# Seven block products in place of eight for half of a down projection's columns, with weight sums made by accumulating DMAs and interleaved with the up projection

## The chip, the core and the metric

The kernel runs on one core of a Trainium2 chip. The metric is the time that the device takes for one execution, in microseconds (us). The profile below is of one such execution, and its times count from the first instruction of the span.

## What is computed

Two decoder layers over 256 tokens of width 2048, all in 32-bit floats. Each layer is a mixer, a convolutional FFN and a gated per-layer embedding, each with a norm ahead of it. The change is in the FFN, which is the larger part of the work:

```python
def conv_ffn(hn, w_up, conv_w, conv_b, w_down):
    u = causal_dwconv(hn @ w_up, conv_w) + conv_b   # w_up 2048 x 11264, conv over 3 tokens
    gate, up = jnp.split(u, 2, axis=-1)
    return (jax.nn.silu(gate) * up) @ w_down        # w_down 5632 x 2048

for i in range(DEPTH):                              # DEPTH 2
    h = h + mixers[i](rmsnorm(h, attn_norms[i]))
    ...
    h = h + conv_ffn(rmsnorm(h, ffn_norm), w_up, conv_w, conv_b, w_down)
```

The mixer of layer 0 matters too, since the change moves buffers that it uses: its first projection (width 5200) gives, in a narrow piece near the start, the two gate inputs of the delta-rule heads (8 columns each), from which `gates()` makes beta and the decay.

## The kernel before

**Precision.** A product of two 32-bit matrices is made of three products of rounded parts: both operands are cut into `hi` (a cast to the rounded form) and `lo` (the rest), and hi·hi, hi·lo and lo·hi are added up in PSUM. A weight chunk of 1 MB comes by one DMA on SP's queue into one of RAWB = 3 `raw` buffers (`load`, L156 to 164), and `split` (L166) cuts it in two pieces of 128x1024: ACT makes `hi` (L179) and DVE makes `lo` = raw − hi (L180). There are WB = 4 buffers each of `hi` and of `lo`. The activations are cut the same way and kept in tiles called `xg`.

**Two gemms.** `gemm_b` (L243 to 260) holds the weights as the stationary operand: a chunk of 8 blocks of 128 by 256 columns takes 16 matmuls of 512 columns (hi against both parts of x, L252), and after a `yield` 16 of 256 columns (lo, L257). The up projection uses it: two chunks for each 256 of its columns. `gemm_a` (L269 to 290) holds the tokens: a chunk of 4 blocks of 128 by 512 columns takes 16 matmuls of 512 columns (L281 and L282, hi) and 8 (L287, lo). The down projection uses it through `proj_add` (L345), which adds the result to the residual tiles `h` on DVE (L351).

**The FFN** (`ffn`, L907) goes by groups of 128-wide blocks of the 44 that d_ff has: (0,4), (4,12), (12,20), (20,28), (28,36), (36,44). For a group, `up` makes two `conv` per pair of blocks: `gemm_b`, then ACT copies the PSUM result (L264) and DVE scales it (L265, L267), ACT makes the first tap of the convolution (L924), DVE adds two taps for each half (L926), and after both, ACT makes silu (L935), DVE multiplies (L936), and ACT and DVE cut the product into `xg` (L356, L357). After a group's `up` stands the whole down projection of the group before it. The last group's down projection comes at the end.

**Order.** Every engine runs its own instructions in an order that is fixed when the program is built: a scheduler orders them from the written program and its dependencies. The pools of buffers (`raw`, `hi`, `lo`, `xg`, PSUM `pa` and `pb`, and T2B = 27 tiles `t` of 128x512) add the waits: a new user of a buffer waits for the last reader of the old one.

**Start of layer 0.** The constants (`cst`, 770.5 KB) and the gates' small tensors (`ab`, `beta`, `gdec`, `eg`, `kdx`, `nbe`) have memory of their own. The narrow piece of the first projection is in PSUM after the first of the gemms of 368 columns, ACT scales it out (L441), and `gates()` follows with three exponentials (L463, L468, L475), a logarithm and another exponential (L484, L488), each of the last two behind a load of ACT's function table.

Of the kernel before, what the change touches and what calls it, by code (L numbers as in the profile page):

```python
# [21 lines left out]
P = 128  # L22
# [7 lines left out]
RAWB = 3  # L30
WB = 4
PSA = 2
PSB = 4
RATES = [1.7, 1.1, 1.1, 0.95, 2.8]
# [48 lines left out]
def trunk(ctx: ExitStack, tc: tile.TileContext, a: dict):  # L83
# [52 lines left out]
    cst = cp.tile([P, N_CST], F32, name="cst", tag="cst")  # L136
# [217 lines left out]

    def put_split(t, k, n, src):
        A.copy(t[:, k : k + n, 0], src)  # L356
        V.tensor_sub(t[:, k : k + n, 1], src, t[:, k : k + n, 0].bitcast(F32))  # L357
# [77 lines left out]
    ab = cp.tile([P, NH, 16], F32, name="ab", tag="ab")  # L435
# [11 lines left out]
    beta = cp.tile([P, HEADS, NH], F32, name="beta", tag="beta")  # L447
    gdec = cp.tile([P, HEADS, NH], F32, name="gdec", tag="gdec")
    eg = cp.tile([P, HEADS, NH], F32, name="eg", tag="eg")
    kdx = cp.tile([P, HEADS, NH], F32, name="kdx", tag="kdx")  # L450
    nbe = cp.tile([P, HEADS, NH], F32, name="nbe", tag="nbe")
# [91 lines left out]
    kp = [cp.tile([P, S], F32, name=f"kp{j}", tag=f"kp{j}") for j in range(2)]  # L543
# [364 lines left out]
    def ffn(l, nf, nxt, aside=None):  # L908
# [9 lines left out]
        def conv(cb, j0):  # L918
            ps = run(gemm_b(w_up, cb, Xf))
# [9 lines left out]
        def up(g0, g1):  # L929
            tiles = []  # L930
            for jp in range(g0, g1, 2):
                tiles.append(xtile())
                yg = conv(jp * P, jp)
                yu = conv(D_FF + jp * P, NFT + jp)
# [3 lines left out]
            return tiles  # L938
# [3 lines left out]
        for g0, g1 in groups:  # L942
            cur = up(g0, g1)
# [4 lines left out]
            if prev is not None:  # L948
                run(proj_add(w_dn, [(prev[0] * P, prev[2], prev[1] - prev[0])], range(CG)))
            prev = (g0, g1, cur)  # L950
# [43 lines left out]
    px = ffn(0, n, ng, lambda: rope_tables(cst[:, C_IRET : C_IRET + 1], cos_r, sin_r, None))  # L994
# [297 lines left out]
```

## Time and profile before

| what | before |
|---|---|
| median of three runs (range) | 2904.06 us (2902.49 to 2905.63) |
| the profiled execution | 2901.51 us |
| its span | 2899.7 us |
| mean granted TensorE clock | 0.999 |
| TensorE busy | 2882.3 us, 99% of the span |
| VectorE (DVE) busy | 1933.0 us, 67% |
| ScalarE (ACT) busy | 1470.1 us, 51% |
| GpSimd (POOL) busy | 64.8 us, 2% |
| DMA | 528.91 MB, mean 182 GB/s |

PE is TensorE's matmuls, PEld its weight loads, which lie beside the matmuls. A mean duration of an instruction includes its latency: instructions of one engine overlap, so their starts stand closer together than their durations. L numbers are lines of the kernel before; in the changed kernel they are moved by 7 at first and by 101 to 133 after `proj_add`.

### The profile page before, as it was taken

What the parts mean: (1) busy time and instruction counts of PE and PEld (TensorE: products, weight loads), DVE (VectorE), ACT (ScalarE), POOL (GpSimd) and SP (SyncE); (2) the same over time, 40 slices, a digit from 0 to 9 for tenths busy, and PEclk for the clock granted to TensorE, in tenths of its full rate; (3) what the DMA queues carried; (4) which work ended last, traced back from release to release, by engine and by line L of the source; (5) the groups of instructions that cost most, each with busy time, mean ns of one, the idle gap of its engine ahead of it and who ended that gap; (6) DMA issues with size and microseconds to landing.
All of it is one profiled execution on the core that took longest, in us unless ns stands there. A gap on an engine that the chain in (4) does not pass through costs nothing.

```text
span 2899.7 us, 38285 instructions
## 1 busy us (share of the span) xinstructions
PE 2882.3 (99%) x15172; PEld 2483.8 (86%) x15172; DVE 1933.0 (67%) x2697; ACT 1470.1 (51%) x2105; POOL 64.8 (2%) x68
## 2 busy tenths in 40 slices
PE   9999999999999999999999999999999999999998
PEld 9899988888888888888888888888888888888887
DVE  7878767777676766556656565665677767666665
ACT  7666645555454544554444443444554544445454
POOL 0111100000000000000000000000000000000000
PEclk9999999999999999999999999999999999999999
DMA  7444355555556555555555555555555555555554
GB/s 241 128 132 141 128 167 182 189 189 189 192 187 198 196 189 191 176 187 187 181 186 183 191 180 186 184 184 189 178 190 192 189 196 189 189 194 188 194 181 162
DMA packets 392117, 528.91 MB, mean 182 GB/s; under 512 B 9216, under 2 KB 265344, under 8 KB 391936
## 3 DMA queue, kind: packets, MB, share of 16 engines
q1 hardware_dynamic: 388512, 521.66, 55.3%
q10 hardware_dynamic: 3424, 4.79, 0.5%
q8 instruction: 119, 1.95, 0.3%
q14 instruction: 62, 0.51, 0.1%
HBM read 524.32 MB, written 2.10 MB: 182 GB/s over the span
## 4 chain that ended last, share of the span: by engine, by line
PE 97%; DVE 1%; DMA 1%; ACT 1%; issue 0%; POOL 0%; ACTq 0%; POOLq 0%; SPq 0%; DVEq 0%
PE pa L252 30%; PE pa L257 16%; PE pa L281 15%; PE pa L282 15%; PE pa L287 14%; PE pb L591 2%; PE pb L301 1%; PE pa L788 1%; DVE lo L180 0%; PE pb L597 0%; PE pb L1031 0%; ACT hi L179 0%; PE pb L233 0%; PE pb L231 0%; PE pb L230 0%
## 5 line engine op out<-in xcount | busy, mean ns | idle before, releaser
L180 DVE TENSOR_TENSOR lo<-raw,hi 128x1024 fp32r<-128x1024 f32 (+3 forms) x1140 | 1200.8, 1075 | 674.3 <-ACT hi L179 614.8
L179 ACT CAST hi<-raw 128x1024 fp32r<-128x1024 f32 (+3 forms) x1140 | 1015.7, 931 | 1087.4 <-PE pa L282 503.9
L252 PE MATMUL pa<-xg,hi 128*128 128x512 f32 x3840 | 927.8, 392 | 0.0
L252 PEld LDWEIGHTS pa<-xg,hi 128*128 128x128 f32 x3840 | 704.5, 188 | 135.6
L281 PE MATMUL pa<-hi,xg 128*128 128x512 f32 (+1 forms) x1924 | 746.6, 388 | 1.0 <-ACT hi L179 1.0
L282 PE MATMUL pa<-hi,xg 128*128 128x512 f32 (+1 forms) x1924 | 744.6, 387 | 0.0
L257 PEld LDWEIGHTS pa<-xg,lo 128*128 128x128 f32 x3840 | 490.3, 191 | 16.3
L257 PE MATMUL pa<-xg,lo 128*128 128x256 f32 x3840 | 502.0, 283 | 0.0
L287 PE MATMUL pa<-lo,xg 128*128 128x512 f32 (+1 forms) x1924 | 473.7, 387 | 0.0
L281 PEld LDWEIGHTS pa<-hi,xg 128*128 128x128 f32 x1924 | 361.7, 188 | 71.3 <-ACT hi L179 1.3
L282 PEld LDWEIGHTS pa<-hi,xg 128*128 128x128 f32 x1924 | 361.5, 188 | 70.1
L287 PEld LDWEIGHTS pa<-lo,xg 128*128 128x128 f32 x1924 | 358.3, 188 | 70.2
L926 DVE SCALAR_TENSOR_TENSOR t<-t,fp,t 128x255 f32<-128x255 f32 (+1 forms) x352 | 161.7, 481 | 108.3 <-ACT t L924 105.2
L264 ACT COPY t<-pa 128x512 f32<-128x512 f32 x128 | 75.1, 587 | 76.8 <-PE pa L257 67.6
L924 ACT ACTIVATE t<-t,fp 128x256 f32<-128x256 f32 x176 | 95.7, 591 | 0.0
L351 DVE TENSOR_TENSOR t<-t,pa 128x512 f32<-128x512 f32 x144 | 92.3, 680 | 3.3 <-PE pa L287 3.3
L152 POOL TENSOR_TENSOR small<-small,mhalf 128x1 f32<-128x1 f32 (+2 forms) x38 | 29.7, 782 | 2653.5 <-DVE small L328 1739.3
L265 DVE TENSOR_TENSOR t<-t,pa 128x512 f32<-128x512 f32 x128 | 87.0, 680 | 1.1 <-ACT t L264 1.1
L306 DVE SCALAR_TENSOR_TENSOR xg<-pb,par,xg 128x256 fp32r<-128x256 f32 x136 | 59.9, 479 | 37.6 <-ACT xg L305 36.8
L267 DVE TENSOR_TENSOR t<-t,rbc 128x512 f32<-128x512 f32 x104 | 73.1, 703 | 0.3
L935 ACT ACTIVATE t<-t 128x512 f32<-128x512 f32 x44 | 27.9, 633 | 71.7 <-DVE t L926 71.7
L305 ACT ACTIVATE xg<-pb,par 128x256 fp32r<-128x256 f32 x136 | 57.8, 469 | 9.3 <-PE pb L301 5.0
(243 smaller groups left out, 1247.7 us busy)
## 6 DMA issues: line engine op xcount, KB each, us to landing
raw<-in_l_ffn_w_up_dram SPq DMA_DIRECT2D x176, 1024.0 KB, 5.1
raw<-in_l_w_in_dram SPq DMA_DIRECT2D x128, 1024.0 KB, 5.2
raw<-in_l_ffn_w_down_dram SPq DMA_DIRECT2D x88, 1024.0 KB, 5.1
raw<-in_l_w_out_dram SPq DMA_DIRECT2D x44, 1024.0 KB, 5.1
raw<-in_l_ple_gate_dram SPq DMA_DIRECT2D x32, 1024.0 KB, 5.2
raw<-in_l_w_in_dram SPq DMA_DIRECT2D x11, 736.0 KB, 4.5
raw<-in_l_mla_w_ukv_dram SPq DMA_DIRECT2D x4, 1024.0 KB, 5.1
raw<-in_l_w_out_dram SPq DMA_DIRECT2D x8, 512.0 KB, 3.9
```

The source lines that it names most:

```text
L179: last_cast[0] = A.copy(vo(hi)[:, c], vi(rk)[:, c])
L180: V.tensor_sub(vo(lo)[:, c], vi(rk)[:, c], vo(hi)[:, c].bitcast(F32))
L252: last_mm[0] = T.matmul(ps[:, j], wh, x2, start=first, stop=False)
L257: last_mm[0] = T.matmul(ps[:, j, :S], lo[k][:, j * P : (j + 1) * P], xr(tiles, c * 8 + k)[1], start=False, stop=c == 1 and k == 7)
L264: A.copy(u, ps[:, :, S:])
L265: V.tensor_add(u, u, ps[:, :, :S])
L281: T.matmul(o[i], xh, hi[k], start=begin and k0 + k == 0, stop=False)
L282: last_mm[0] = T.matmul(o[i], xw, hi[k], start=False, stop=False)
L287: last_mm[0] = T.matmul(o[i], xl(tiles, k0 + k, i)[0], lo[k], start=False, stop=end and k0 + k == nkb - 1)
L351: V.tensor_add(h[i][c], h[i][c], ps[:, i])
L924: A.activation(y[:, j], u[:, j], AF.Identity, scale=fc(ct + 176), bias=fc(ct + 264))
L926: V.scalar_tensor_tensor(y[:, j, lag:], u[:, j, : S - lag], fc(ct + (2 - lag) * 88), y[:, j, lag:], op0=ALU.mult, op1=ALU.add)
```

## The change

Five things are done, all in one edit.

1. **Seven products.** For the four middle groups of each layer (eight blocks of 128), and for columns 0 to 1023 of the down projection, the product is treated as one of 2x2 blocks: two halves of the tokens, two halves of the inner dimension, two halves of the columns. A recursion with seven block products in place of eight is used. A block product is 12 matmuls of 512 columns (4 blocks of 128, three parts each).
2. **Forms of the activations** (`Forms`): four sums and differences of activation blocks, made for each four blocks of 128 by four DVE instructions of 128x256 and cut into hi and lo by two ACT casts and two DVE subtractions of 128x512.
3. **Sums of the weights.** Five of the seven products need sums or differences of weight blocks. They are held in one running sum in two `xg` tiles and in one `raw` slab: a plain DMA on SP's queue (`put`) writes the first block and an accumulating DMA on POOL's queue (`plus`) adds the next one. Each such DMA moves 512 KB. Per seven there are 8 accumulating and 10 plain ones (9 MB); the old code loaded 4 chunks of 1 MB there. After a sum is ready, `cut` makes its hi and lo as for any chunk.
4. **Interleaving.** `up` and the new `down` are generators. The down projection of the group before no longer stands behind a group's `up`; it is taken along with it: after LAG = 6 steps of `up`, 0.9 steps of `down` for each of the 42 that are left. `down` does columns 1024 to 2047 by `gemm_a` first and then the seven. It uses PSUM `pb` and not `pa`. The first group's down projection is interleaved too, without the seven; the last group's stays as it was.
5. **Room.** RAWB is 4, but one of the four buffers is `slab` until the end of layer 0's mixer: it now holds `cst` and the gates' small tensors. One column of `cst` that is needed later is copied to a tile of its own (`iret`).

The core of the diff:

```diff
-RAWB = 3
+RAWB = 4
+LAG = 6
+SHARE = 0.9
...
-    cst = cp.tile([P, N_CST], F32, name="cst", tag="cst")
+    slab = rawp.tile([P, 2048], F32, tag="raw", name="slab")
+    cst = slab[:, :N_CST]
+    iret = cp.tile([P, 1], F32, name="iret", tag="iret")
...
     def split(src, k, n, views=None):
         raw = ahead.pop() if ahead else load(src, k, n)
+        return cut(raw, k, n, views)
+
+    def cut(raw, k, n, views=None):
...
+        def add(self, y0, y1):
+            a11, a21, a12, a22 = y0[:, :, :P], y0[:, :, P:], y1[:, :, :P], y1[:, :, P:]
+            f = [t2((P, 2, 2, P)) for _ in range(2)]
+            s1, s2, s3, s4 = f[0][:, 0], f[0][:, 1], f[1][:, 0], f[1][:, 1]
+            V.tensor_sub(s1, a22, a21)
+            V.scalar_tensor_tensor(s2, s1, -1.0, a11, op0=ALU.mult, op1=ALU.subtract)
+            V.tensor_sub(s3, a11, a21)
+            V.scalar_tensor_tensor(s4, a12, -1.0, s2, op0=ALU.mult, op1=ALU.subtract)
+            hi = [t2((P, 2, 2, P), F32R) for _ in range(2)]
+            lo = [t2((P, 2, 2, P), F32R) for _ in range(2)]
+            for j in range(2):
+                A.copy(hi[j], f[j])
+                V.tensor_sub(lo[j], f[j], hi[j].bitcast(F32))
...
+        def put(dst, hh, e):
+            for q in range(2):
+                nc.sync.dma_start(dst[q], blocks[q, hh, e])
+
+        def plus(dst, hh, e):
+            for q in range(2):
+                G.dma_start(dst[q], blocks[q, hh, e], accum_op=ALU.add)
...
+        def product(o, left, right, start):
+            los = []
+            for q in range(2):
+                hi, lo = cut(right[q], 2, 512)
+                los.append(lo)
+                for k in range(2):
+                    l = left(q, k)
+                    T.matmul(o, l[0], hi[k], start=start and q + k == 0, stop=False, skip_group_check=True)
+                    last_mm[0] = T.matmul(o, l[1], hi[k], start=False, stop=False, skip_group_check=True)
+                yield
+            for q in range(2):
+                for k in range(2):
+                    last_mm[0] = T.matmul(o, left(q, k)[0], los[q][k], start=False, stop=q + k == 2, skip_group_check=True)
+            yield
+
+        h11, h12, h21, h22 = h[0][c], h[0][c + 1], h[1][c], h[1][c + 1]
+        run_t = [xtile().bitcast(F32).rearrange("p a b c -> p a (b c)") for _ in range(2)]
+        put(run_t, 0, 0)
+        plus(run_t, 0, 1)
+        yield
+        A_, B_, C_ = pb(), pb(), pb()
+        yield from product(C_, forms.left(0), run_t, True)
+        V.tensor_sub(h22, h22, C_)
+        plus(run_t, 1, 1)
+        yield from product(A_, x(0, 0), fresh(0, 0), True)
+        V.tensor_add(h11, h11, A_)
+        t3 = slab()
+        put(t3, 0, 1)
+        plus(t3, 1, 1)
+        yield from product(B_, x(1, 0), fresh(1, 0), True)
+        V.tensor_add(h11, h11, B_)
+        yield from product(A_, forms.left(1), run_t, False)
+        V.tensor_sub(h12, h12, A_)
+        plus(run_t, 1, 0)
+        yield from product(C_, forms.left(3), fresh(1, 1), False)
+        V.tensor_sub(h12, h12, C_)
+        yield from product(A_, forms.left(2), t3, False)
+        V.tensor_sub(h22, h22, A_)
+        yield from product(A_, x(1, 1), run_t, False)
+        V.tensor_add(h21, h21, A_)
...
-    ab = cp.tile([P, NH, 16], F32, name="ab", tag="ab")
+    ab = kept(256, 32).rearrange("p (i g) -> p i g", i=NH)
...
         for g0, g1 in groups:
-            cur = up(g0, g1)
+            forms = Forms() if 0 < g0 and g1 < NFT else None
+            cur = (g0, g1, [], forms)
+            going = up(g0, g1, cur[2], forms)
+            if prev is not None:
+                behind_it = down(*prev)
+                for _ in range(LAG):
+                    next(going)
+                owed = 0.0
+                for _ in going:
+                    owed += SHARE
+                    while owed >= 1.0:
+                        owed -= 1.0
+                        next(behind_it, None)
+                run(behind_it)
+            else:
+                run(going)
...
-            if prev is not None:
-                run(proj_add(w_dn, [(prev[0] * P, prev[2], prev[1] - prev[0])], range(CG)))
```

**Start of layer 0, ACT.** The rows of ACT from the casts for the second gemm of 368 columns on, before: `hi` are pieces of weights that this gemm needs, `ab` and `t` are the narrow piece out of the first gemm's PSUM, `rbc` is part of the norm.

```order
L179 CAST hi_408<-raw_406 128x368 x2
L179 CAST hi_414<-raw_406 128x368 x2
L179 CAST hi_450<-raw_448 128x368 x2
L441 ACTIVATE ab<-pa_143,small_377 128x16
L441 ACTIVATE t_60_382<-pa_143,small_377 128x352
L441 ACTIVATE ab<-pa_143,small_377 128x16
L441 ACTIVATE t_61_383<-pa_143,small_377 128x352
L179 CAST hi_456<-raw_448 128x368
L340 COPY rbc_430<-pb_428 128x256
```

The same place in the changed kernel, where `slab` is also `ab`:

```order
L546 ACTIVATE slab<-pa_144,small_378 128x16
L546 ACTIVATE t_60_382<-pa_144,small_378 128x352
L546 ACTIVATE slab<-pa_144,small_378 128x16
L546 ACTIVATE t_61_383<-pa_144,small_378 128x352
L568 ACTIVATE small_562<-small_562 128x16
L573 ACTIVATE small_567<-small_567 128x16
L580 ACTIVATE small_575<-small_573 128x16
L589 ACT_TABLE_LOAD
L589 ACTIVATE small_584<-small_577 128x16
L593 ACT_TABLE_LOAD
L593 ACTIVATE small_588<-alog 128x8
L186 CAST hi_404<-raw_402 128x368 x2
```

The casts that the second gemm needs stood ahead of the copies out of the first gemm's result; now they stand behind those copies, the three exponentials, both table loads, the logarithm and the last exponential.

**Within a seven, PE.** Before, rows at the end of an up chunk and the beginning of the down projection of group (4,12), whose matmuls (L281, L282) then run on for 16 chunks in a row:

```order
L257 MATMUL pa_6119<-xg_5022,lo_6169 128x256 x2
L257 MATMUL pa_6119<-xg_5032,lo_6169 128x256 x2
L281 MATMUL pa_6252<-hi_6255,xg_5002 128x512
L282 MATMUL pa_6252<-hi_6255,xg_5002 128x512
L281 MATMUL pa_6252<-hi_6255,xg_5002 128x512
L282 MATMUL pa_6252<-hi_6255,xg_5002 128x512
```

In the changed kernel, rows where the sixth product of the first seven of layer 0 ends (L428, into `pb_6932`), an up chunk's lo half follows (L264), and the seventh product begins in the same PSUM tile (L423, L424):

```order
L428 MATMUL pb_6932<-lo_7353,t_1100_5979 128x512 x2
L428 MATMUL pb_6932<-lo_7379,t_1160_6387 128x512 x2
L264 MATMUL pa_7296<-xg_4958,lo_7363 128x256 x2
L264 MATMUL pa_7296<-xg_4968,lo_7363 128x256 x2
L264 MATMUL pa_7296<-xg_5017,lo_7367 128x256 x2
L264 MATMUL pa_7296<-xg_5027,lo_7367 128x256 x2
L264 MATMUL pa_7296<-xg_4958,lo_7363 128x256 x2
L264 MATMUL pa_7296<-xg_4968,lo_7363 128x256 x2
L264 MATMUL pa_7296<-xg_5017,lo_7367 128x256 x2
L264 MATMUL pa_7296<-xg_5027,lo_7367 128x256 x2
L423 MATMUL pb_6932<-hi_7415,xg_5689 128x512
L424 MATMUL pb_6932<-hi_7415,xg_5689 128x512
```

Down and up now alternate, and between a product and the next in the same PSUM tile stand 16 matmuls of 256 columns.

**The same place, DVE.** Before, rows of DVE in a down projection (L351 adds to `h`, L180 makes lo pieces):

```order
L351 TENSOR_TENSOR t_798_4179<-t_798_4179,pa_7188 128x512
L351 TENSOR_TENSOR t_799_4181<-t_799_4181,pa_7188 128x512
L180 TENSOR_TENSOR lo_7301<-raw_7294,hi_7300 128x1024
L180 TENSOR_TENSOR lo_7334<-raw_7331,hi_7333 128x1024
L180 TENSOR_TENSOR lo_7338<-raw_7331,hi_7337 128x1024
L180 TENSOR_TENSOR lo_7368<-raw_7365,hi_7367 128x1024
L351 TENSOR_TENSOR t_800_4183<-t_800_4183,pa_7259 128x512
L351 TENSOR_TENSOR t_801_4185<-t_801_4185,pa_7259 128x512
L180 TENSOR_TENSOR lo_7372<-raw_7365,hi_7371 128x1024
```

In the changed kernel, at the place of the PE rows above: L187 is a lo piece, L1042 and L459 belong to the activation, L453 takes the sixth product out of `pb_6932`:

```order
L187 TENSOR_TENSOR lo_7353<-raw_7105,hi_7352 128x1024
L1042 TENSOR_TENSOR t_1283_7149<-t_1283_7149,t_1303_7284 128x512
L187 TENSOR_TENSOR lo_7363<-raw_7360,hi_7362 128x1024
L187 TENSOR_TENSOR lo_7367<-raw_7360,hi_7366 128x1024
L459 TENSOR_TENSOR xg_7008<-t_1283_7149,xg_7008 128x2x256
L187 TENSOR_TENSOR lo_7379<-raw_7105,hi_7378 128x1024
L187 TENSOR_TENSOR lo_7416<-xg_6908,hi_7415 128x1024
L453 TENSOR_TENSOR t_801_4180<-t_801_4180,pb_6932 128x512
L187 TENSOR_TENSOR lo_7438<-raw_7435,hi_7437 128x1024
L187 TENSOR_TENSOR lo_7442<-raw_7435,hi_7441 128x1024
L272 TENSOR_TENSOR t_1324_7423<-t_1324_7423,pa_7296 128x512
```

Before, only lo pieces and adds to `h` stood in a down projection; now the up projection's activation work stands between them, and the instruction that empties `pb_6932` stands behind `lo_7416`, the first lo piece of the seventh product.

## Rows read from the trace of the kernel before

**Rows 1.** The page's head: the span, the busy time of each engine with its share of the span and its count of instructions, the clock that TensorE was granted in 40 equal slices (tenths of full speed), and the chain of work that ended last by engine.

```profile
span 2899.7 us, 38285 instructions
PE 2882.3 (99%) x15172; PEld 2483.8 (86%) x15172; DVE 1933.0 (67%) x2697; ACT 1470.1 (51%) x2105; POOL 64.8 (2%) x68
...
PEclk9999999999999999999999999999999999999999
...
PE 97%; DVE 1%; DMA 1%; ACT 1%; issue 0%; POOL 0%; ACTq 0%; POOLq 0%; SPq 0%; DVEq 0%
```

**Rows 2.** What TensorE waited for: total us, times, longest. The whole span has ten such rows; the first and the fifth stand here, and the last line is the only one in the FFN of layer 0 (480 to 1170 us).

```profile
PE pb L585 <- DVE t L704: 1.6, 1, 1.6
...
PE pb L301 <- DVE t L506: 0.8, 1, 0.8
...
PE pb L338 <- DVE t L334: 0.2, 1, 0.2
```

**Rows 3.** Busy time by stretch (us from the span's start: length, PE, PEld, DVE, ACT, POOL busy with their instructions, granted clock, DMA share, GB/s): nearly the whole FFN of layer 0; its first 40 us, with the rope tables of layer 1 in them; a stretch of up projection alone; and one of down projection alone, whose matmuls all have 512 columns.

```profile
480.00:1170.00 690.00, 689.81 (x3706) 598.36 (x3705) 485.56 (x638) 348.35 (x441) 1.54 (x1) 1.00 0.58 190
480.00:520.00 40.00, 39.81 (x230) 34.79 (x229) 38.57 (x71) 23.94 (x40) 1.54 (x1) 1.00 0.53 171
689.00:721.00 32.00, 32.00 (x188) 28.33 (x187) 23.91 (x33) 17.87 (x24) 0.00 (x0) 1.00 0.56 179
733.00:760.00 27.00, 27.00 (x120) 22.35 (x120) 16.19 (x18) 10.53 (x11) 0.00 (x0) 1.00 0.61 200
```

**Rows 4.** Groups of instructions in 480 to 1170 us, by line and shape (busy us, mean ns of one, then idle time before them and what ended it).

```profile
L252 PE MATMUL pa<-xg,hi 128*128 128x512 f32 x1408 | 336.5, 391 | 0.0
L180 DVE TENSOR_TENSOR lo<-raw,hi 128x1024 fp32r<-128x1024 f32 x249 | 302.4, 1221 | 131.8 <-ACT hi L179 131.7
L179 ACT CAST hi<-raw 128x1024 fp32r<-128x1024 f32 x248 | 253.9, 1047 | 269.3 <-PE pa L252 117.4 <-PE pa L282 82.8 <-issue 68.7
L282 PE MATMUL pa<-hi,xg 128*128 128x512 f32 x292 | 113.7, 389 | 0.0
L926 DVE SCALAR_TENSOR_TENSOR t<-t,fp,t 128x255 f32<-128x255 f32 x88 | 42.2, 481 | 50.9 <-ACT t L924 50.9
L265 DVE TENSOR_TENSOR t<-t,pa 128x512 f32<-128x512 f32 x44 | 29.9, 681 | 0.0
L351 DVE TENSOR_TENSOR t<-t,pa 128x512 f32<-128x512 f32 x42 | 26.9, 680 | 0.5 <-PE pa L287 0.5
L357 DVE TENSOR_TENSOR xg<-t,xg 128x512 fp32r<-128x512 f32 x22 | 15.2, 692 | 19.0 <-ACT xg L356 19.0
L356 ACT CAST xg<-t 128x512 fp32r<-128x512 f32 x22 | 13.5, 613 | 4.8 <-DVE t L936 4.8
L373 DVE SCALAR_TENSOR_TENSOR t<-t,t 128x256 f32<-128x256 f32 x15 | 6.4, 424 | 0.4
```

**Rows 5.** Waits of DVE and of the SP queue in the same stretch (total us, times, longest).

```profile
DVE lo L180 <- ACT hi L179: 131.7, 55, 3.2
SPq L163 <- DVE lo L180: 619.2, 122, 8.8
```

**Rows 6.** DMA: issues by source with count, KB each and median us from issue to landing (whole span; 1024 KB, then 512 KB); the share of 16 engines that SP's queue took from 500 to 1160 us; and busy time of the first stretch of the program, for the DMA share and GB/s at its end.

```profile
raw<-in_l_ffn_w_down_dram SPq DMA_DIRECT2D x88, 1024.0 KB, 5.1
raw<-in_l_ple_proj_dram SPq DMA_DIRECT2D x8, 512.0 KB, 3.8
q1 hardware_dynamic: 104686, 125.20, 58.2%
12.00:16.00 4.00, 3.10 (x20) 2.79 (x18) 1.84 (x4) 2.31 (x6) 0.00 (x0) 1.00 1.05 382
```

**Rows 7.** The timeline around the second piece of the first projection of layer 0 (start us, us, what, [idle before]): ACT, and then the two rows of PE at which the first gemm of 368 columns ends and the second begins.

```profile
28.19 2.50 ACT L179 CAST hi<-raw 128x368 fp32r<-128x368 f32 x6
30.58 0.28 ACT L441 ACTIVATE ab<-pa,small 128x16 f32<-128x16 f32 x1
31.35 0.58 ACT L441 ACTIVATE t<-pa,small 128x352 f32<-128x352 f32 x1
31.78 0.53 ACT L179 CAST hi<-raw 128x368 fp32r<-128x368 f32 x1
...
34.45 0.24 ACT L463 ACTIVATE small<-small 128x16 f32<-128x16 f32 x1
34.68 0.23 ACT L475 ACTIVATE small<-small 128x16 f32<-128x16 f32 x1
...
38.64 1.28 ACT L484 ACT_TABLE_LOAD   x1
39.94 0.22 ACT L484 ACTIVATE small<-small 128x16 f32<-128x16 f32 x1
40.17 1.28 ACT L488 ACT_TABLE_LOAD   x1
41.47 0.21 ACT L488 ACTIVATE small<-alog 128x8 f32<-128x8 f32 x1
41.58 1.69 ACT L179 CAST hi<-raw 128x368 fp32r<-128x368 f32 x4
...
28.84 1.51 PE L287 MATMUL pa<-lo,xg 128*128 128x368 f32 x8
30.20 0.33 PE L281 MATMUL pa<-hi,xg 128*128 128x368 f32 x1
```

More of the change, by code (lines that the diff above doesn't have):

```diff
@@ new lines, in seven, with slab, fresh, x @@
+    def seven(w, r0, c, tiles, forms):
+        blocks = w[r0 : r0 + 8 * P, c * 512 : (c + 2) * 512].rearrange("(q h k p) (e n) -> q h e p k n", q=2, h=2, k=2, e=2)
+        def put(dst, hh, e):
[4 more added lines that the diff above has]
+                G.dma_start(dst[q], blocks[q, hh, e], accum_op=ALU.add)
+        def slab():
+            raw = rawp.tile([P, 4, 512], F32, tag="raw", name=nm("raw"))
+            return [raw[:, 2 * q : 2 * q + 2] for q in range(2)]
+        def fresh(hh, e):
+            dst = slab()
+            put(dst, hh, e)
+            return dst
+        def x(half, i):
+            def at(q, k):
+                return xl(tiles, 4 * q + 2 * half + k, i)
+            return at
+        def product(o, left, right, start):
[37 more added lines that the diff above has]
+        V.tensor_add(h21, h21, A_)
@@ L541, in rope64 @@
         V.tensor_add(dst, dst, t)
-    kp = [cp.tile([P, S], F32, name=f"kp{j}", tag=f"kp{j}") for j in range(2)]
+    kp = [kept(0, S), cp.tile([P, S], F32, name="kp1", tag="kp1")]
     def make_kp():
@@ L927, in conv, with up @@
             return y
-        def up(g0, g1):
-            tiles = []
+        def up(g0, g1, tiles, forms):
+            kept = []
             for jp in range(g0, g1, 2):
                 tiles.append(xtile())
-                yg = conv(jp * P, jp)
-                yu = conv(D_FF + jp * P, NFT + jp)
+                yg = yield from conv(jp * P, jp)
+                yu = yield from conv(D_FF + jp * P, NFT + jp)
                 A.activation(yg, yg, AF.Silu)
@@ L937, in up, with down @@
                 put_split(tiles[-1], 0, 2, yg)
-            return tiles
+                if forms is not None:
+                    kept.append(yg)
+                    if len(kept) == 2:
+                        forms.add(*kept)
+                        kept = []
+        def down(g0, g1, tiles, forms):
+            r0, nk = g0 * P, g1 - g0
+            for c in range(0 if forms is None else 2, CG):
+                ps = [pb() for _ in range(NH)]
+                yield from gemm_a(w_dn, r0, nk, c * 512, 512, tiles, ps)
+                for i in range(NH):
+                    V.tensor_add(h[i][c], h[i][c], ps[i])
+            if forms is not None:
+                yield from seven(w_dn, r0, 0, tiles, forms)
         groups = [(max(g - 4, 0), g + 4) for g in range(0, NFT, 8)]
```

29 lines of the change are left out of this document (21 added, 8 removed).

## The prediction

> **What bounds the kernel now.** I read the page's head first. TensorE (PE) is busy for 99% of the span, at full clock in all slices, and 97% of the chain that ended last is PE [rows 1]. The table of its waits comes next: it is short, no wait is longer than 1.6 us, and in the FFN of layer 0 there is one, of 0.2 us [rows 2]. So time there is the number of matmuls by their price, and whatever takes matmuls away shortens the kernel if the others keep up. How near they are is read by stretch. In 690 us of FFN, PE is busy for 689.8, DVE for 485.6 (70%), ACT for 348.4 (50%), and DMA is at 0.58 [rows 3]. Their order is a ring: the queue of loads waits for DVE to free a raw buffer, DVE waits for ACT's hi pieces, and ACT mostly waits for PE to free a hi buffer [rows 4, 5]. PE pulls all of them.
>
> **Matmuls removed.** The stretch of down projection has 120 matmuls in 27.00 us, so one of 512 columns costs 0.225 us [rows 3]. Each seven has 7 x 12 = 84 in place of 96, and there are four in each of two layers: 96 matmuls less, 96 x 0.225 = **21.6 us** saved. Their weight loads lie beside them. The mean duration of 0.389 us [rows 4] would be the wrong price, since matmuls overlap.
>
> **The start of layer 0.** Here the order matters. Before, PE ended the first gemm and began the next at 30.20 us, because the casts that it needed had been done from 28.19 on, ahead of the copies out of PSUM [rows 7]. Now those casts stand behind the copies and the whole of `gates()` on ACT. The copies can't start before the first gemm has ended, at about 30.5 (30.58 before). Four take to 31.78, that is 1.2 us. A first DVE step and three exponentials end about 32.3 (from 34.45 to 34.8 three take 0.35). The first table load and the logarithm take 40.17 − 38.64 = 1.53, the second and its exponential 41.58 − 40.17 = 1.41. The first cast (0.53 for one alone) ends near 35.5. PE, which would have gone on at 30.20, waits **5.2 us**. Nothing hides it: it is in the order of one engine. DVE's own rows there (gates and rope) are about 25 of 0.1 to 0.4 us and end before lo is needed, 16 matmuls later. Bounds: 4, if DVE's step lies under the copies; 7, if the logarithm waits for DVE between. Some 0.8 us may come back, because the wait at L506 [rows 2] is for a result of those gates.
>
> **Clock.** After such a gap the granted clock, which is 1.00 in every stretch here [rows 1, 3], may fall to the lower of its two levels. No row of before has PE idle so long, so none prices it. Matmuls at half clock cost double: a fall that lasts as long as the gap loses 2.6 us, and I keep 0 to 2.6 for the range, with 0 in the sum. The Trainium skill's "TensorE: Matmul & The Clock Gate", section "Why this matters for your kernels", says that idle gaps between bursts of matmuls bring the half clock back; by it the sum would be 2.6 more. No row here decides it.
>
> **DVE within a seven.** The 22 steps of a seven go with 22 / 0.9 = 24.4 steps of up, three to a chunk: 8.15 chunks. The up stretch had 188 matmuls in 32.00 us [rows 3], 32 to a chunk, so 5.45 us each. The phase lasts 8.15 x 5.45 + 84 x 0.225 = 44.4 + 18.9 = 63.3 us. DVE has in it: 75% of 44.4 (23.91 of 32.00 [rows 3]) = 33.2; 14 lo pieces of 1.22 = 17.1; 7 adds to h of 0.68 = 4.8; one set of forms, 4 of 0.42 and 2 of 0.68 = 3.0 [rows 4]. Together 58.1 us, 92%, where a down projection had 60% (16.19 of 27.00 [rows 3]). In one stretch before, DVE was 96% busy (38.57 of 40.00) and PE lost 0.19 us [rows 3]. So it fits, without much room, and single late pieces are to be expected. Two places have little slack. The seventh product goes on in the PSUM tile of the sixth, which DVE must first read; between stand 16 matmuls of 256 columns, 5.45 − 16 x 0.225 = 1.85 us, but on DVE one lo piece (1.22) and the read (0.68) = 1.90 plus latency: late by up to 0.5. And the lo piece for the end of the sixth stands behind the activation's multiply and cut (0.68 + 0.69). I take 0.5 us per seven, **4 us** in all, with 0 and 1.5 per seven (12 in all) as ends.
>
> **ACT, PSUM, first and last groups.** ACT has 56% of 44.4 (17.87 of 32.00 [rows 3]) = 24.9, 14 casts of 1.05 = 14.7 and two of the forms at 0.61 [rows 4]: 40.8 of 63.3 us, so it has room. The interleaving itself removes no matmul. It lets a down projection end up to a group later, with nothing reading `h` before the FFN's end: nothing.
>
> **DMA within a seven.** From 500 to 1160 us 125.20 MB took 58.2% of 660 us: 3.07 us for 1 MB. At the start 382 GB/s went at a share of 1.05: 2.75 us [rows 6]. A phase moves 8.15 up chunks and 10 plain transfers of 512 KB, 13.8 MB, and 4.2 MB that accumulate. If an accumulated byte costs as much as a copied one, that is 49 to 55 us of 63.3 (78 to 87%). If it costs double, 61 to 68 us (96 to 108%). No row shows an accumulating DMA, so its price stays between copy and three copies; I take one to one and a half, with the lateness in the 4 us above. An accumulation itself may be late: from its issue to its product lie 20 us or more, by the order of PE's rows, against 3.8 us for a plain one of 512 KB [rows 6]. What can suffer is the 1 MB loads that share the engines, 5.1 us now. POOL, which issues the new DMAs, is 2% busy [rows 1].
>
> **Sum.** 2901.5 (the profiled execution; its span is 2899.7) − 21.6 + 5.2 + 4 = 2889.1. The median of the runs shown lies 2.5 above that execution, so 2889 to 2892: I say **2890**.
>
> **Rivals.**
> *Accumulating DMAs starve the loads (slower).* At double price and 3.07 us per MB a phase needs 68.1 us of DMA in 63.3: 4.8 us lost per seven; at 2.75, nothing. The middle, 2.4 x 8 = 19, gives 2908, the far end 2927. It decides from 2 us per seven, where 21.6 − 5.2 is eaten: by 3.07, accumulation at 1.8 times a copy. For it: the loads wait for DVE, so there is no stock beyond the raw buffers, one of which holds a sum. Against: over a whole group (16 up chunks, 4 of down, a seven: 128 us, 30.4 MB) the share is 73%. Chance 0.2. The Trainium skill's "Collectives: The Full Stack", section "The bandwidth ceiling: the fold count and why AG ≠ RS ≠ AR", says that an add in the DMA path costs nothing itself but needs two source reads where a copy needs one; by it the price is double, and this rival has the middle number.
> *DVE becomes the bound in the phases.* In 690 us DVE waited 131.7 for hi pieces [rows 5]; at 92% there is no place for such waits, and a late hi makes a late lo. At 2 to 3 us per seven: 2901 to 2909. Against: the stretch at 96%. Chance 0.15.
> *The start doesn't wait, or the sevens lose nothing.* 2880 to 2885. Chance 0.1.
> *The clock falls after the start's gap* and the forecast holds otherwise: 2892. Chance 0.15.
> *The change doesn't do what it says.* The counts of matmuls in PE's order exclude it.
>
> **How the numbers follow.** The forecast (2885 to 2892) has 0.40. With the third and fourth rival, 0.65 lie below 2898. Within 0.2% of before (5.8 us, about what a measurement of this kernel tells from no change) lie half of the first two, 0.17; 0.18 end above 2910. The range reaches from full savings without a stall, 2879, into the first rival, to 2914: outside are its far end and what I haven't seen. The forecast's own range is 2884 to 2896.
>
> **What would show it.** Right: one PE wait of some 5 us near 31 us on ACT's first hi of the second gemm, and the other waits of the first mixer as they were; in the FFN waits of PE summing to 2 us per layer, on lo pieces or on PSUM `pb`, DVE above 88% in the phases; accumulations that land within 10 us and 1 MB loads within 7. Wrong: PE waits on hi pieces that wait for a DMA (first rival), or on lo pieces at DVE above 97% (second). A start with the casts issued ahead would take 5 us from the forecast.

## The result, and the profile after

| kernel | median us | ratio to before, 95% interval |
|---|---|---|
| before | 2904.0 | 1 |
| changed | 2913.2 (2912.1 to 2914.5) | 1.0032 (1.0021 to 1.0043) |
| changed, second set of runs | 2912.2 (2909.5 to 2915.9) | 1.0029 (1.0017 to 1.0041) |

The change makes the kernel 0.3% slower, 8 to 9 us, where 14 us less were forecast. The first profiled execution ran at a granted clock of 0.653 from end to end, so the trace below is one of the second set. TensorE (PE) has 96 matmuls less and 10.6 us less of busy time than in [rows 1], and yet the span is 14 us longer (this execution lies 3.8 us above the median of its set, that of [rows 1] 2.5 below its own). The time is in waits: PE is idle for 42.4 us, where it was for 17.4. The page's head, and PE's longest totals of waits:

```profile
span 2914.1 us, 38688 instructions
PE 2871.7 (99%) x15076; PEld 2467.9 (85%) x15076; DVE 2036.7 (70%) x2866; ACT 1533.5 (53%) x2185; POOL 141.4 (5%) x132
...
PE pa L264 <- DVE lo L187: 9.2, 8, 1.7
PE pb L428 <- DVE lo L187: 7.9, 7, 2.3
PE pa L288 <- ACT hi L186: 7.2, 2, 5.4
PE pa L894 <- DVE t L272: 2.0, 1, 2.0
```

In [rows 2] the FFN of layer 0 had one wait, of 0.2 us. Now 17 us of waits for lo pieces are in the sevens, about two waits in each (first two rows), and one of 5.4 us is at the start (within the third row). The DMA rows of the same trace:

```profile
q0 software_dynamic: 17408, 33.56, 6.6%
...
raw<-in_l_ffn_w_up_dram SPq DMA_DIRECT2D x176, 1024.0 KB, 5.6
...
raw<-in_l_ffn_w_down_dram SPq DMA_DIRECT2D x64, 512.0 KB, 5.8
...
xg<-in_l_ffn_w_down_dram POOLq DMA_DIRECT2D x48, 512.0 KB, 8.5
...
raw<-in_l_ffn_w_down_dram POOLq DMA_DIRECT2D x16, 512.0 KB, 10.8
```

A plain transfer of 512 KB, of another weight, took 3.8 us before [rows 6]. Those of the sevens take 5.8, and the accumulating ones 8.5 to 10.8. (Where the accumulating ones only copy, in b below, the plain ones still take 5.1.) One late piece, followed back: PE's wait of the first seven (first row), ACT behind a raw block (second), and what SP and POOL had issued by then (start us, span of the row's issues, [idle before <- releaser]).

```profile
732.88 1.69 PE L264 MATMUL pa<-xg,lo 128*128 128x256 f32 x12 [1.72 <-DVE lo L187]
...
728.40 1.05 ACT L186 CAST hi<-raw 128x1024 fp32r<-128x1024 f32 x1 [4.98 <-DMA raw<-in_l_ffn_w_down_dram]
...
710.20 10.21 SPq L396 DMA_DIRECT2D raw<-in_l_ffn_w_down_dram  x4
...
711.61 2.43 POOL L400 DMA_DIRECT2D xg<-in_l_ffn_w_down_dram  x2 [20.98 <-DVE lo L187]
715.73 2.50 POOL L400 DMA_DIRECT2D raw<-in_l_ffn_w_down_dram  x2 [1.69 <-DMA raw<-in_l_ffn_w_down_dram]
```

Read from below: two accumulations of the running sum start at 711.6, two of the slab's sum at 715.7, and among four plain blocks of SP's queue ACT waits 4.98 us for one. ACT's hi, DVE's lo and PE's wait of 1.72 us follow.

### The profile page after: what moved, and what is told of

Read it like the earlier page. It is cut to its first block, busy times and chain, and to the rows that moved or that the text cites. A ratio compares the mean times of both kernels' runs of the same rounds, so it can differ in the third digit from the quotient of the medians.

```text
span 4078.7 us, 38688 instructions
## 1 busy us (share of the span) xinstructions
PE 4061.2 (100%) x15076; PEld 2898.7 (71%) x15076; DVE 2068.0 (51%) x2866; ACT 1578.9 (39%) x2185; POOL 140.3 (3%) x132
## 3 DMA queue, kind: packets, MB, share of 16 engines
q0 software_dynamic: 17408, 33.56, 4.8%
## 4 chain that ended last, share of the span: by engine, by line
PE 99%; ACT 0%; issue 0%; DMA 0%; DVE 0%; ACTq 0%; POOLq 0%; POOL 0%
PE pa L259 31%; PE pa L264 15%; PE pa L288 11%; PE pa L294 11%; PE pa L289 11%; PE pb L289 3%; PE pb L294 3%; PE pb L288 3%; PE pb L697 2%; PE pb L428 2%; PE pb L424 2%; PE pb L423 2%; PE pb L308 1%; PE pa L894 1%; PE pb L703 0%; PE pb L1164 0%
## 5 line engine op out<-in xcount | busy, mean ns | idle before, releaser
L187 DVE TENSOR_TENSOR lo<-raw,hi 128x1024 fp32r<-128x1024 f32 (+3 forms) x1140 | 1195.5, 1076 | 1302.1 <-ACT hi L186 860.1
L259 PE MATMUL pa<-xg,hi 128*128 128x512 f32 x3840 | 1328.1, 508 | 0.0
L259 PEld LDWEIGHTS pa<-xg,hi 128*128 128x128 f32 x3840 | 793.1, 210 | 412.6 <-issue 134.0
L264 PEld LDWEIGHTS pa<-xg,lo 128*128 128x128 f32 x3840 | 656.2, 237 | 50.9 <-issue 17.7
L288 PE MATMUL pa<-hi,xg 128*128 128x512 f32 (+1 forms) x1348 | 680.0, 505 | 5.4 <-ACT hi L186 5.4
L289 PE MATMUL pa<-hi,xg 128*128 128x512 f32 (+1 forms) x1348 | 675.3, 501 | 0.2 <-DVE xg L313 0.2
L264 PE MATMUL pa<-xg,lo 128*128 128x256 f32 x3840 | 675.4, 344 | 0.0
L288 PEld LDWEIGHTS pa<-hi,xg 128*128 128x128 f32 x1348 | 282.0, 209 | 154.6 <-issue 50.6
L289 PEld LDWEIGHTS pa<-hi,xg 128*128 128x128 f32 x1348 | 279.1, 207 | 147.6 <-issue 45.3
L294 PEld LDWEIGHTS pa<-lo,xg 128*128 128x128 f32 x1348 | 277.3, 207 | 147.1 <-issue 46.6
L289 PE MATMUL pb<-hi,xg 128*128 128x512 f32 x348 | 176.8, 508 | 0.0
L288 PE MATMUL pb<-hi,xg 128*128 128x512 f32 x348 | 175.7, 505 | 0.0
L294 PE MATMUL pb<-lo,xg 128*128 128x512 f32 x348 | 122.3, 506 | 0.0
L289 PEld LDWEIGHTS pb<-hi,xg 128*128 128x128 f32 x348 | 74.2, 213 | 37.6 <-issue 14.4
```

Source lines behind the costliest of these rows:

```text
L187: V.tensor_sub(vo(lo)[:, c], vi(rk)[:, c], vo(hi)[:, c].bitcast(F32))
L259: last_mm[0] = T.matmul(ps[:, j], wh, x2, start=first, stop=False)
L264: last_mm[0] = T.matmul(ps[:, j, :S], lo[k][:, j * P : (j + 1) * P], xr(tiles, c * 8 + k)[1], start=False, stop=c == 1 and k == 7)
L288: T.matmul(o[i], xh, hi[k], start=begin and k0 + k == 0, stop=False)
L289: last_mm[0] = T.matmul(o[i], xw, hi[k], start=False, stop=False)
L294: last_mm[0] = T.matmul(o[i], xl(tiles, k0 + k, i)[0], lo[k], start=False, stop=end and k0 + k == nkb - 1)
```

## Experiments

### The parts of the change

**a_again**, the changed kernel, is above. **b_plain_pool** adds nothing up: the transfers on POOL's queue copy.

```diff
-                G.dma_start(dst[q], blocks[q, hh, e], accum_op=ALU.add)
+                G.dma_start(dst[q], blocks[q, hh, e])
```

**c_slab_only** is the kernel before with `slab`, `iret`, `kept` and RAWB = 4 alone. **d_eight_interleaved** is the changed kernel with `forms = None` for all groups: interleaved, with eight products.

> The changed kernel once more, for a trace at full clock. Where the forecast said 2890 us and the timed runs say 2913, some 24 us are to be found. Theory 1 (accumulating DMAs starve the loads): PE waits in the sevens on hi pieces whose raw chunk landed late; 1 MB loads in the phases land after 7 us or more. Theory 2 (DVE bound): PE waits on lo pieces or on PSUM pb, DVE above 97% busy in the phases. Theory 3 (the clock): the mean granted clock is 0.997 where it was 0.999, and the rows at the lower level stand behind gaps of PE; 0.002 of 2911 us is 6 us. All expect one wait of some 5 us at the start.

> The 64 transfers on POOL's queue copy in place of adding, so the sums of weights are left out; bytes, queue, order and the instructions of all engines are the same. If the accumulation's price is what holds the sevens (theory 1), this is some 15 to 25 us faster than the changed kernel, near 2890. If the loads are late for the bytes alone or DVE is the bound (theory 2), it is within 3 us of it, near 2912.

> The kernel before with only the move of the constants and of the gates' tensors into a raw buffer. My term for it: 5.2 us more than before, 2909, with one PE wait of some 5 us near 31 us. If the clock falls behind that gap, up to 2.6 more. If four raw buffers later on are worth something, less.

> The changed kernel with eight products for all columns: no forms, no sums of weights, no transfers on POOL's queue, but the down projection interleaved with up as before, and the constants in the raw buffer. If interleaving itself costs nothing, it is as the kernel with only the moved constants, about 2909. If what the sevens lose comes from interleaving (waits on PSUM pb or lo pieces because activation work stands between), it is 10 us or more above that, 2920.

| kernel | median us | ratio to before |
|---|---|---|
| b_plain_pool | 2891.1 | 0.9957 (0.9940 to 0.9973) |
| c_slab_only | 2912.2 | 1.0027 (1.0017 to 1.0036) |
| d_eight_interleaved | 2912.4 | 1.0028 (1.0018 to 1.0039) |

This takes the change apart. The slab costs 8.6 us (c − before), the interleaving nothing (d − c, 0.2), seven products with free sums save 21.3 (d − b), and the accumulation takes 21.1 back (a − b). Waits in the sevens are gone in b; the head of its page, the row that is left of those waits, its POOL queue, and a stretch of seven and up in b and then in the changed kernel:

```profile
span 2888.8 us, 38688 instructions
...
PE pb L428 <- DVE lo L187: 0.4, 1, 0.4
...
q0 software_dynamic: 9216, 33.56, 3.4%
...
xg<-in_l_ffn_w_down_dram POOLq DMA_DIRECT2D x48, 512.0 KB, 6.0
...
710.00:770.00 60.00, 60.00 (x320) 51.89 (x319) 50.54 (x67) 37.64 (x46) 4.34 (x6) 1.00 0.80 263
```

```profile
711.00:775.00 64.00, 60.69 (x319) 51.74 (x318) 50.45 (x67) 37.61 (x46) 7.21 (x6) 1.00 0.88 246
```

The same 33.56 MB take 3.4% of 2889 us when copied, 2.93 us for a MB, and 6.6% of 2914 us when added, 5.73: **1.96 times** by these rounded shares. DVE is 84% busy in b's phase (50.54 of 60.00), and PE loses nothing there.

The late block of the section above shows how that price reaches PE. First its row on ACT in b, and the DMA of the nine us around it there (718 to 727: packets, MB and share of the 16 engines; q1 is SP's queue, q0 POOL's), then the same of the changed kernel (719 to 728):

```profile
723.10 1.05 ACT L186 CAST hi<-raw 128x1024 fp32r<-128x1024 f32 x1 [0.85 <-DMA raw<-in_l_ffn_w_down_dram]
...
q1 hardware_dynamic: 1380, 1.90, 62.3%
q0 software_dynamic: 168, 0.58, 16.1%
...
raw<-in_l_ffn_w_down_dram SPq DMA_DIRECT2D x2, 512.0 KB, 5.2
```

```profile
q0 software_dynamic: 716, 1.38, 83.6%
q1 hardware_dynamic: 414, 0.81, 26.0%
...
raw<-in_l_ffn_w_down_dram SPq DMA_DIRECT2D x2, 512.0 KB, 9.4
```

In the changed kernel the two queues together have 110% of the engines in these nine us, most of it for the accumulations. SP's queue moves 0.81 MB where it moved 1.90, the two plain blocks take 9.4 us in place of 5.2, and ACT's wait is 4.98 us in place of 0.85. The 88% of the whole phase hides such a stretch.

The start, in c: PE's first matmuls behind the wait, and the stretches around it (PE, PEld, DVE, ACT, POOL, granted clock, DMA share, GB/s).

```profile
36.14 0.67 PE L283 MATMUL pa<-hi,xg 128*128 128x368 f32 x1 [5.44 <-ACT hi L181]
36.61 0.51 PE L284 MATMUL pa<-hi,xg 128*128 128x368 f32 x1
36.91 0.51 PE L283 MATMUL pa<-hi,xg 128*128 128x368 f32 x1
...
30.00:36.00 6.00, 0.70 (x5) 0.39 (x3) 4.05 (x24) 5.05 (x13) 0.00 (x0) 0.95 0.01 3
36.00:42.00 6.00, 5.86 (x18) 5.68 (x19) 5.83 (x15) 4.16 (x11) 0.00 (x0) 0.50 0.46 129
42.00:48.00 6.00, 6.00 (x36) 6.00 (x36) 5.26 (x14) 2.60 (x6) 0.00 (x0) 0.98 0.64 187
```

PE waits 5.44 us, and behind the gap the granted clock is 0.50 until 42 us: a matmul of 368 columns starts 0.31 us after the one before, where it was 0.17 (30.20 to 30.36 in the trace before). From 36.1 to 42 that is about 3 us of work lost, and 5.4 + 3.0 make up most of the 8.6 measured. The split isn't exact: the trace has another 1.9 us of waits for hi in the first mixer (1.0 before), and PE's busy time grew by only 1.3 us, since in the first 16 us, ahead of the gap, it is 1.4 us less in c's trace (12.06 against 13.46).

### What an accumulation costs

**q_double_plain** sends each accumulated block as two copies on the same queue; **r_start2** is its base, and **p_floor** has single copies (and the slab's sum started later, as in k below). r_start2 mends the start: two chunks of the second narrow gemm are written ahead of the copies out of the first.

```diff
-        ps = run(first_gemm if g3 == 0 else gemm_a(w_in, 0, KB, 4096 + 368 * g3, 368, X))
+        ps = run(first_gemm if g3 == 0 else coming)
+        if g3 == 0:
+            coming = gemm_a(w_in, 0, KB, 4096 + 368, 368, X)
+            for _ in range(4):
+                next(coming)
+        elif g3 == 1:
+            coming = gemm_a(w_in, 0, KB, 4096 + 736, 368, X)
```

> The changed kernel with only the second mended start: two chunks of the next gemm written ahead of the copies, everything in the sevens as in the change. The start's 8 us come back and the sevens lose what they lost: 2902 to 2905, the same as before. It is the base for the two below.

> As r_start2, with each accumulating transfer replaced by two plain copies of the same block on POOL's queue, so that the sums are left out. By the profiles an accumulated MB takes 5.7 us of the 16 engines and a copied one 2.9, so two copies take as much engine time as one accumulation. If engine time is the whole price of accumulating: the same as r_start2 within 4 us. If accumulating hurts in another way (its own latency, the reads of the memory that DVE and ACT use), it is faster by 10 us or more, near the plain kernel's 2883.

> As l_late_sum_start2, with the 64 transfers on POOL's queue copying in place of adding: the sums of weights are left out. What is left between the two is the price of the accumulation where it no longer meets the other sum. Burst theory: under 5 us. Price everywhere: 10 us or more. It should be near 2882, which is 2901.5 less 21.6 and 2 us around it.

r_start2: 2906.5 us, 1.0008 (0.9998 to 1.0017), so that the new start gives back 5.7 us of the 8.6; q_double_plain: 2929.3, 1.0086 (1.0069 to 1.0102); p_floor: 2883.5, 0.9935 (0.9922 to 0.9949). The POOL queue of q, its PE's longest waits and a stretch behind one of them, and PE's waits in r:

```profile
q0 software_dynamic: 18432, 67.12, 6.6%
...
PE pa L259 <- ACT hi L186: 18.2, 9, 2.4
PE pb L429 <- DVE lo L187: 9.7, 5, 2.3
...
762.00:767.00 5.00, 5.00 (x25) 4.53 (x24) 4.81 (x6) 2.45 (x4) 0.00 (x0) 0.66 1.09 361
```

```profile
PE pa L264 <- DVE lo L187: 9.7, 8, 1.7
PE pb L428 <- DVE lo L187: 4.4, 6, 1.7
```

Two copies take the share that one accumulation takes (6.6%), and they hurt more: q is 23 us slower than r, where the same within 4 us was expected. So engine time without any addition is enough to lose what the accumulations lose, but equal engine time isn't an equal loss. q waits in other places (for hi of up chunks, at L259, with the clock below 1.00 behind such waits), and its second copy of a block is issued only when the first has landed (711.72 behind 705.31 for the first block of its first seven). That the addition costs nothing but engine time is therefore not shown. p_floor shows what is behind it, 20.4 us under before.

### Which loads are late

Three guesses at how to live with that traffic, all on **e_start_fixed** (a first mending of the start: one step of the gemm ahead, the gates behind its casts): thinner phases (**f_thin**, LAG 2 and SHARE 0.75), denser phases (**j_dense**, SHARE 1.3), and the two sums apart (**k_late_sum**: `t3`, its `put` and `plus` moved behind the third product). **l_late_sum_start2** is k with the start of r_start2.

> The changed kernel with the order at the start put back: the first step of the next gemm of 368 columns is written ahead of the copies out of the first one, and the gates are issued behind that gemm's casts. The start cost 5.4 us of waiting and some 3 us at half clock behind it. Theory (start and sevens are separate losses): 8 us faster than the changed kernel, 2904, with the granted clock at 1.00 from 30 to 45 us. If the gap only moves to the gates' later users, no gain: 2912.

> As e_start_fixed, and the sevens spread over more of up: LAG 2, SHARE 0.75. A phase then has 22 / 0.75 / 3 = 9.8 up chunks, 72 us in place of 63, and at 5.7 us for a MB that accumulates and 3.07 for one that is copied its DMA need falls from 105% to 98%. If saturated DMA is what makes the loads late, most of the 20 us come back: 2886 to 2894. If each accumulation hurts whenever it runs, whatever else does, within 4 us of e_start_fixed.

> As e_start_fixed, with SHARE 1.3: a phase has 5.6 up chunks, 50 us, DMA need 118%, and DVE at about 95%. Saturated DMA expects the loss to grow by the DMA time that doesn't fit, 9 us a phase in place of 3: slower than e_start_fixed by 20 to 50 us. If each accumulation has a fixed price, the same as e_start_fixed within 4 us.

> As e_start_fixed (2908), but the sum in the raw slab (t3) is started after the third product in place of after the second, so that its two accumulations don't run beside those of the running sum. Theory of the burst: in the changed kernel DMA stands idle for some 4 us and then four plain and four accumulating transfers of 512 KB start within 6 us, and the chunk behind them is late; apart, they don't hurt: waits of PE in the sevens fall from 18 us to under 6, 2893 to 2897. Rival (the accumulated bytes cost the same wherever they run): within 4 us of 2908.

> As k_late_sum, with another order at the start: two chunks of the next gemm are written ahead of the copies, and the gates are not held back behind the rest. It should have neither the wait of 5.4 us at the start nor the one of 2.8 us on the transposes that wait for the gates: 4 to 6 us faster than k_late_sum. If the sum's burst is the cause, 2886 to 2892 and faster than before.

| kernel | median us | ratio to before |
|---|---|---|
| e_start_fixed | 2908.0 | 1.0013 (1.0003 to 1.0022) |
| f_thin | 2928.7 | 1.0087 (1.0071 to 1.0103) |
| j_dense | 2942.8 | 1.0134 (1.0119 to 1.0149) |
| k_late_sum | 2931.1 | 1.0097 (1.0083 to 1.0110) |
| l_late_sum_start2 | 2928.8 | 1.0087 (1.0074 to 1.0101) |

e got back 4 of the 8 us; the gates came too late instead, a wait of 2.8 us. Only j came as expected. Thinner phases were worse, though the DMA share of the first seven is 0.79 in f (702 to 778) against 0.88, so the mean need of DMA isn't what decides; the sums apart were worse too, so neither is their collision. What l has is one long wait in each seven. Its PE, the load behind it on ACT, and the stretch after:

```profile
743.24 3.68 PE L259 MATMUL pa<-xg,hi 128*128 128x512 f32 x8 [3.98 <-ACT hi L186]
...
742.14 3.89 ACT L186 CAST hi<-raw 128x1024 fp32r<-128x1024 f32 x4 [8.06 <-DMA raw<-in_l_ffn_w_up_dram]
...
744.00:746.00 2.00, 2.00 (x7) 1.54 (x6) 1.58 (x2) 2.00 (x4) 0.00 (x0) 0.50 0.03 10
```

An up chunk keeps ACT waiting 8.06 us and PE 3.98, and the clock is at 0.50 behind it, so that the wait costs more than itself. The eight waits of this line are 29.0 us together; p_floor, the same order with copies, is 45 us faster. Two further runs change the order or the adder: **s_spread** (the two products without a sum first, the chunks of columns 1024 to 2047 between the others) and **h_pool_adds** (plain load into a raw buffer, `G.tensor_tensor` in place of `G.dma_start`).

> As r_start2, with the seven spread over the whole down projection: the two products that need no sum come first, the chunks of columns 1024 to 2047 stand between and beside the later products, and the raw slab's sum is started apart from the others. DMA need of the stretch falls from 105% to about 86%, and DVE's load from 92% to some 80%. If the loads were late because the phases are full, PE's waits in the sevens fall under 5 us in all: 2884 to 2890, faster than both. If each accumulation delays the one load that stands beside it whatever the mean load is, four delays per seven remain: 2900 or more.

> As e_start_fixed, but the second block of each sum is loaded by a plain DMA on SP's queue into a raw buffer and added on POOL, 8 additions of 128x1024 per seven. DMA need falls to that of the kernel with plain copies (2891, and 8 less for the start: 2883). Against it: each sum holds a raw buffer for the load and the addition, and POOL and DVE may slow one another. If POOL's additions take under 5 us each and disturb nobody, 2883 to 2890; if raw buffers or DVE suffer, above 2904.

s_spread: 2908.0 us, 1.0013 (1.0004 to 1.0023), against its base r_start2 no better, as the second of its two theories had it: 13 us of waits for hi remain, at other places. h_pool_adds: 2988.6, 1.0289 (1.0271 to 1.0306). POOL's additions:

```profile
L406 POOL TENSOR_TENSOR xg<-xg,raw 128x1024 f32<-128x1024 f32 x48 | 136.5, 2864 | 1094.0 <-DMA raw<-in_l_ffn_w_down_dram 680.9 <-DVE lo L187 217.8 <-ACT hi L186 195.3
L406 POOL TENSOR_TENSOR raw<-raw,raw 128x1024 f32<-128x1024 f32 x16 | 80.4, 5044 | 63.5 <-DMA raw<-in_l_ffn_w_down_dram 63.5
```

They take 2.9 and 5.0 us, about what was hoped for, but each keeps a raw buffer, up chunks come late (54 us of ACT's waits in layer 0's FFN), and DVE's busy time grows from 2035.7 us (in e) to 2099.8 with the same 2866 instructions. Which of the two costs more isn't shown.

### Less of that traffic

The slab's sum on DVE: ahead of the third product as in the change (**u_dve_sum_early**), just ahead of the sixth (**u_dve_sum_late**), ahead of the fifth (**w_dve_sum_mid**); and late, with the running sum's last step on DVE too (**x_two_dve_sums**). All have the start of r_start2.

```diff
-        t3 = slab()
+        t3, other = slab(), slab()
         put(t3, 0, 1)
-        plus(t3, 1, 1)
+        put(other, 1, 1)
+        for q in range(2):
+            V.tensor_add(t3[q], t3[q], other[q])
...
-        plus(run_t, 1, 0)
+        last = slab()
+        put(last, 1, 0)
+        for q in range(2):
+            V.tensor_add(run_t[q], run_t[q], last[q])
```

> As r_start2 (2906), with the sum in the raw slab made on DVE, from two plain loads, in place of by accumulation: 6 accumulating transfers per seven in place of 8. DMA need of a phase falls by 3 us of 66, and the two accumulations that stood beside the running sum's are gone; DVE gets 2.3 us of 63 more (92 to 96%). If engine time beside the raw loads is the price: PE's waits in the sevens fall by a third or more, 2895 to 2902. If DVE's room is short: 2906 to 2915, with lo pieces late and no DMA behind them.

> As u_dve_sum_early, with the slab's sum loaded and added just ahead of the sixth product, so that no raw buffer is held by it for 40 us. Four buffers in place of three for the loads in most of the phase: their lateness is borne better, 2890 to 2898, faster than before. If the late chunk is always one that flies beside the running sum's accumulations, within 3 us of u_dve_sum_early.

> As u_dve_sum_late (2899), with the slab's sum loaded and added one product earlier, ahead of the fifth. There DVE waited 3.6 us at its addition for the block's load, with the lo pieces of others behind it. If that wait in order is what the remaining 12 us of PE waits come from: 2890 to 2896. If the buffers held for one product more cost as much, 2899 to 2904.

> As u_dve_sum_late, with the last step of the running sum made on DVE as well: 4 accumulating transfers per seven, DVE 2.3 us more (near 99% of a phase). If traffic beside the loads is still the price: 2890 to 2896. If DVE or the raw buffers are now what ends last: 2902 to 2912.

| kernel | median us | ratio to before |
|---|---|---|
| u_dve_sum_early | 2904.4 | 1.0003 (0.9994 to 1.0013) |
| u_dve_sum_late | 2899.1 | 0.9985 (0.9976 to 0.9994) |
| w_dve_sum_mid | 2936.6 | 1.0106 (1.0089 to 1.0123) |
| x_two_dve_sums | 2891.1 | 0.9955 (0.9940 to 0.9969) |

x beats both kernels, and came as expected; the two u runs and w lie outside both of the ranges named for each. x's span, what is left of PE's waits in the sevens, its POOL queue, its first seven (701 to 762) and another stretch of 60 us that begins within it:

```profile
span 2889.4 us, 38651 instructions
...
PE pa L259 <- ACT hi L186: 3.8, 3, 2.0
PE pb L423 <- ACT hi L186: 1.4, 5, 0.3
...
q0 software_dynamic: 8704, 16.78, 3.3%
...
701.00:762.00 61.00, 60.64 (x319) 51.65 (x318) 55.96 (x73) 38.20 (x47) 2.43 (x2) 1.00 0.84 255
707.00:767.00 60.00, 59.64 (x314) 50.79 (x313) 58.68 (x75) 35.77 (x45) 0.00 (x0) 1.00 0.79 244
```

DVE is 92% busy in the seven and 98% in the other stretch, and PE loses 0.36 us in either. The slab's two loads one product earlier, in w, cost 37 us more than in u_dve_sum_late. SP's queue, two accumulations and ACT in w, and the landing of the chunk that ACT waits for:

```profile
720.54 8.24 SPq L396 DMA_DIRECT2D raw<-in_l_ffn_w_down_dram  x6
735.18 14.69 SPq L167 DMA_DIRECT2D raw<-in_l_ffn_w_up_dram  x4
...
730.71 1.19 POOL L400 DMA_DIRECT2D xg<-in_l_ffn_w_down_dram  x1 [25.07 <-DVE t L1040]
733.42 1.19 POOL L400 DMA_DIRECT2D xg<-in_l_ffn_w_down_dram  x1 [1.52 <-issue]
...
743.70 1.04 ACT L186 CAST hi<-raw 128x1024 fp32r<-128x1024 f32 x1 [9.60 <-DMA raw<-in_l_ffn_w_up_dram]
...
raw<-in_l_ffn_w_up_dram SPq DMA_DIRECT2D x1, 1024.0 KB, 8.4
```

Six blocks of the down projection, three raw buffers, go in a row, and the next up chunk can only be issued at 735.18, when a buffer is free again: 9.60 us of waiting for ACT. Even then it takes 8.4 us, beside two accumulations issued at 730.71 and 733.42, where the median is 5.2. So a load is late for two reasons, the traffic on the engines and the buffers that stand ahead of it. w differs from u_dve_sum_late only in the second by its edit, but its late chunk has both, and no run here has the second alone. In f_thin's first seven the two plain blocks beside the slab's accumulations take 9.1 us, no more than the 9.4 of the changed kernel; what differs is that PE waits 4.29 us behind them, with the clock below 1.00 after it, where 1.7 was the longest at that line in e. Why the same lateness reaches PE further there is open.

## Why the prediction was wrong

**Matmuls, 21.6 us saved**: right, d − b is 21.3. The 0.225 us came from the busy time of a stretch, not from the mean duration.

**The start, 5.2 us**: the order showed the wait, and 5.44 us came. What failed is the clock: I put 0 in the sum, and about 3.0 came. The trace before had no gap long enough to show it. The Trainium skill's "TensorE: Matmul & The Clock Gate", "Why this matters for your kernels", had said it, and c's row of 0.50 agrees; by it the term would have been 7.8 of 8.6.

**DVE within a seven, 92%**: too high. Mean durations were added up, but instructions of DVE overlap, and the phase had 236 matmuls of up, 7.4 chunks, not 8.15. Measured: 84% in b, 79% in the changed kernel. The 4 us of small waits were 0.4 without the accumulation, and the second rival falls: in the changed kernel PE waits for lo pieces though DVE is far from full, and in x, with DVE at 92 to 98%, PE loses under 1%, as the stretch of 96% in [rows 3] had said.

**ACT, PSUM, interleaving at nothing**: right within the noise, d − c is 0.2.

**DMA within a seven**: the step that failed. "I take one to one and a half, with the lateness in the 4 us above": it was 1.96 copies, and the lateness 18 us of waits, 21 in time (2.6 a seven). This was the first rival, with a chance of 0.2; its 2 us a seven, from which it decides, were passed. The Trainium skill's "Collectives: The Full Stack", "The bandwidth ceiling: the fold count and why AG ≠ RS ≠ AR", had the price right: two source reads, twice a copy. That the rival's middle number, 2.4 us a seven, came so near was luck, for the way to it failed too: it took the need of a whole phase against its length, and the phase has a share of 88% (711 to 775), with 6 and not 8 of a seven's accumulations in it; thinning the phases didn't help either. The shortage is local, 110% in nine us, and single loads are late, beside the traffic and behind held buffers, which a budget for a phase doesn't see.

With these terms the sum is 2904.0 − 21.6 + 8.6 + 21 = 2912.0, against 2912.2; as 8.6 and 21 are differences of the same runs, this confirms only the term of the matmuls. Of the signs named, the wait at 31 us came; accumulations landed at 8.5 to 10.8 us, about the 10 named. The loads of 1 MB landed at 5.6 in the median of the whole span, but at 7.1 in the first seven (5.4 in b's), past the 7 named:

```profile
raw<-in_l_ffn_w_up_dram SPq DMA_DIRECT2D x9, 1024.0 KB, 7.1
```

The signs of the two rivals failed: PE waited on lo pieces at DVE 79%, which neither named, since ACT's hi, late for a DMA, makes the lo late. A median hides the one late load in each seven: the signs should have been ACT's waits for DMA.

## What to carry to other kernels

Traffic that costs DMA engine time must be weighed at the loads that fly beside it and at the buffers that they wait for, not by a mean share: a pipeline with three buffers turns one late load into a wait of the engine that sets the time. Look at the share in stretches of some microseconds around a late load. If a change can bring a gap into a TensorE that never idles, price the gap with the matmuls behind it at half clock. And take a change apart into its parts on the chip: here two losses of 9 and 21 us hid a gain of 21, and moving half of the sums to an engine that looked full (DVE) and mending one order at the start gave a kernel 0.45% faster.

## What the runs showed of the hardware that I had not expected

- An accumulating DMA from HBM into SBUF took 5.73 us of the 16 engines for a MB where a copy took 2.93, with 17408 packets in place of 9216. In the nine us from 719 the accumulations had 83.6% of the engines and SP's loads beside them 26.0%.
- Behind a gap of 5.4 us the granted clock was 0.50 for some 7 us, 6 of them with matmuls running; behind the wait of 3.98 us in the sevens (l) it fell too, while in the changed kernel the one of 1.72 us at 732.88 left it at 1.00.
- Additions of 128x1024 on POOL took 2.9 to 5.0 us, and DVE's own instructions became slower beside them: 64 us more of busy time over 64 additions.
